# Matmul pieces laid beside a convolution and its LayerNorm, and weight sums on VectorE, in a one-core encoder layer

## The chip, the cores and the metric

The kernel runs on one core of a Trainium2 chip. The metric is the time of one execution on the device in microseconds (us). Engine names are those of the profile: PE is TensorE (matmuls), PEld its weight loads, DVE VectorE, ACT ScalarE, POOL GpSimd, SP the engine that issues most DMAs (`nc.sync`). A DMA that POOL issues (`G.dma_start` with `accum_op`) adds what it reads to what lies at its destination.

## The reference

One layer of a bidirectional encoder, S = 1024 positions, D = 1024, all in float32:

```
h  = rmsnorm(x);  P = h @ w_in                   # 8192 columns, split among the mixers
a  = glu(P[conv]);  a = depthwise_conv31(a)      # 512 channels, centred, 31 taps
a  = silu(layernorm(a)) @ pw_w                   # 512 -> 1024
o  = bidirectional_gated_scan(q, v, z_f, z_b)    # 8 heads of 128, chunks of 64
b  = (rmsnorm(o) * silu(og)) @ o_w
x  = x + (sigmoid(gA) * a + sigmoid(gB) * b) @ w_out
x  = x + (silu(dwconv3(h2 @ w_gate)) * (h2 @ w_up)) @ w_down    # h2 = rmsnorm(x), 2816 wide
out = rmsnorm(x)
```

## The kernel before

**Matmuls.** Every float32 product is three matmuls: each operand is split into a rounded high part and a rest (`split`, L121: ACT copies the high part, DVE subtracts it), and `mm3` (L146 to L148) adds high by high, rest by high and high by rest in one PSUM bank. A matmul is 128x128 weights by 512 positions; the two halves of the positions are `half` 0 and 1.

**Pair jobs.** Two columns of weights at a time are multiplied in Strassen's manner: seven products in place of eight, each of twelve matmuls, in the order 1, 2, 6, 7, 5, 4, 3 (`pair_job`, L316). For this the weights have to be added up first. `rows` (tile `wr`) is a column's weights, `col` (tile `sw`) gets the sum of both columns' upper parts, and then `wr` is changed in place by two sums (`sums`, L340). The function `add` (L329) makes these: for the first pair (`first`) DVE does, with the second column's weights loaded as another `wr`; for all others POOL issues an accumulating DMA. The order of weights is: products 1 and 2 split from `rows` as loaded (tile `wp`), 7 and 5 from `col` (tile `wq`), 6 and 3 from `rows` after the sums (tile `wp` again), 4 from a fourth part (tile `w`). A pair's results leave PSUM by DVE: (0, 0) after product 2 from bank `tr`, (1, 1) after product 5 (`ev<-su,mm`), (1, 0) after product 4 (`ev<-sc,su`), (0, 1) after product 3. ACT copies three products aside (`su`, L385). Product 3 is written to the same bank `mm` from which (1, 1) is read.

**Buffers.** `wr` has two, `sw` one, `wp` four, `wq` three, `su` four, the matmul bank `mm` three, `sc` and `tr` two each, `ob` one.

**Order.** What PE does is in the order in which the program emits it. The matmuls of a stream of jobs are generators that yield after six matmuls, here called a piece; `Stream.fill(n)` emits the next n pieces (fractions add up). A pair has 14 pieces, the 16 pairs of the input projection 224. The order on the other engines is a scheduler's, from the emitted order, the buffers and its own estimates.

**Around the change.** `s_pairs` is the stream of the 16 pairs (`in_pair`, L765). The depthwise convolution (`conv_steps`, L962) is 4 groups of channels by 31 taps, each tap one DVE instruction of 128x1024 (L970 or L973); after each, `CONV_FILL` pieces are emitted. Sums of the convolution (`acc`) go out to DRAM by `d_cv` and come back by `cx`. Then comes the LayerNorm, once for each half of the positions: six pieces, then the mean (PE L1000), DVE takes it off (L1002), six pieces, squares on ACT (L1006), sums of them (L985, L987), the variance (PE L546, a DVE copy to `r` at L550, POOL's L527 and L528, four small scalings of an identity on ACT, L535), `fill(3)`, the spread over partitions (PE L536, ACT L537), then scale, offset, silu and the split to `ch` (L1013 to L1017), and 14 pieces. The eight pointwise jobs (`conv_pw_w`) of that half are put in at the head of the queue, behind those of the half before. What is left is drained at the end (L1028).

**The FFN.** Its 22 pairs (`ffn_job`, L1580) use the same `pair_job`, `late=True`, the first of them with `now`, which takes its sums earlier. All their sums are by POOL's DMAs.

Of the kernel before, what the change touches and what calls it, by code (L numbers as in the profile page):

```python
# [17 lines left out]

P = 128
FILL = 1.37  # L20
CONV_FILL = 1.6
NPAIRS = 16
LN_FILL = 6
LN_LAST = 14
GLU_FIRST = 4
# [20 lines left out]
def tile_hybrid_encoder(  # L46
# [84 lines left out]
    def raw_w(src, nk):  # L131
        t = mp.tile([P, nk, P], F32, tag="wr", name=nm("wr"), bufs=2)
        nc.sync.dma_start(t, src)
        return t
# [178 lines left out]

        return prep, run

    def pair_job(src0, src1, nk, acts, wpool, pool, evac, su=4, first=False, late=False, now=False):  # L316

        def steps(w):
            def both(src, alt, late=late):
                hi, lo = split(w_page(2 * nk, alt), w_page(2 * nk, alt), src, V, late)
                return [(hi[:, :nk], lo[:, :nk]), (hi[:, nk:], lo[:, nk:])]

            def add(o, a):  # L329
                if first:  # L330
                    V.tensor_tensor(o, o, a, op=ALU.add)
                else:
                    G.dma_start(o, a, accum_op=ALU.add)  # L333

            rows = raw_w(src0, 2 * nk)
            col = wpool.tile([P, 2 * nk, P], F32, tag="sw", name=nm("sw"), bufs=1)
            nc.sync.dma_start(col[:, :nk], src0[:, :nk])
            nc.sync.dma_start(col[:, nk:], src1[:, :nk])
            add(col, raw_w(src1, 2 * nk) if first else src1)
            def sums():  # L340
                add(rows[:, :nk], col[:, nk:])
                add(rows[:, nk:], rows[:, :nk])

            def quadrant():
                a22 = pool.tile([P, nk, P], F32, tag="w4", name=nm("w4"), bufs=1)
                nc.sync.dma_start(a22, src1[:, nk:])
                return a22

            if now:
                w[1], w[2] = both(rows, None, False)  # L350
                sums()
                yield 0
                w[6], w[3] = both(rows, None, False)
                yield 1
                a22 = quadrant()
                yield 2
                w[7], w[5] = both(col, pool)
                yield 4
            else:
                yield 4  # L360
                w[1], w[2] = both(rows, None)
                sums()
                a22 = quadrant()
                yield 6
                w[7], w[5] = both(col, pool)
                yield 3
                w[6], w[3] = both(rows, None)
                yield 3
            one = w_page(2 * nk, pool)
            w[4] = split(one[:, :nk], one[:, nk:], a22, V, late)  # L370

        def prep():
            w = Weights(steps)
            return w if late else w.all()

        def run(w):
            def product(i, acc, fresh=True):
                for k in range(nk):
                    mm3(acc, w[i], acts(i)[k], k, fresh and k == 0, k == nk - 1, not fresh)
                    if k % 2 == 1 or k == nk - 1:  # L380
                        yield

            def copy(acc):
                t = page(pool, "su", su)
                A.copy(t, acc)  # L385
                return t

            row, b2, col = bank("mm"), bank("tr"), bank("sc")
            yield from product(1, row)
            p1 = copy(row)  # L390
            yield from product(2, b2)
            evac(0, 0, b2, p1, ALU.add)
            yield from product(6, row, False)
            u2 = copy(row)
            yield from product(7, col)
            p7 = copy(col)
            yield from product(5, row, False)
            evac(1, 1, p7, row, ALU.subtract)
            yield from product(4, col, False)
            evac(1, 0, col, u2, ALU.subtract)  # L400
            yield from product(3, row, False)
            evac(0, 1, row)

        return prep, run
# [360 lines left out]
    def in_pair(n):  # L765
        (c0, e0), (c1, e1) = todo[2 * n], todo[2 * n + 1]
        evs = (e0, e1)
        return pair_job(
            in_cols(c0),
            in_cols(c1),  # L770
            NK2,
            lambda i: ht[i],
            p1,
            p1,
            lambda e, *quadrant: evs[e](*quadrant),
            first=n == 0,
        )

    gate = {}
# [176 lines left out]


    jobs = collections.deque(in_pair(n) for n in range(1, NPAIRS))
    jobs.appendleft((lambda: w_pair0, pair0[1]))
    s_pairs = Stream(run_jobs(jobs, 4))  # L960
# [19 lines left out]
    for _ in conv_steps():  # L980
        s_pairs.fill(CONV_FILL)

# [8 lines left out]
    for half in range(2):  # L991
        xs = []
        for j in range(NCW):
            if j % 2 == 0:
                both = p1.tile([P, 2, H], F32, tag="ca", name=nm("cx"), bufs=2)
            nc.sync.dma_start(both[:, j % 2, :], d_cv[j][half])
            xs.append(both[:, j % 2, :])
        s_pairs.fill(LN_FILL)
        mean = bank("ob")
        T.matmul(mean, ones_m, total(xs, tmp()), start=True, stop=True)  # L1000
        for t in xs:
            V.scalar_tensor_tensor(t, mean, -1.0 / CW, t, op0=ALU.mult, op1=ALU.add)  # L1002
        s_pairs.fill(LN_FILL)
        sqs = [tmp() for _ in xs]
        for sq, t in zip(sqs, xs):
            A.activation(sq, t, AF.Square)  # L1006
        rstd = rstd_over_partitions(total(sqs, sqs[0]), CW, "ob", tmp())
        next(rstd)
        s_pairs.fill(3)
        rs = next(rstd)  # L1010
        ca = []
        for j, xn in enumerate(xs):
            V.tensor_tensor(xn, xn, rs, op=ALU.mult)  # L1013
            V.tensor_scalar(xn, xn, vec("lnw", j), vec("lnb", j), op0=ALU.mult, op1=ALU.add)
            A.activation(xn, xn, AF.Silu)
            both = gp0.tile([P, 2, H], F32R, tag="gl", name=nm("ch"), bufs=NCW)
            ca.append(split(both[:, 0, :], both[:, 1, :], xn, V))  # L1017
        s_pairs.fill(LN_LAST)
        at = 0
        while at < len(jobs) and jobs[at] in pw_jobs:  # L1020
            at += 1
        for i in range(ND):
            job = std_job(
                w_cols(conv_pw_w, 0, NCW, i * P), NCW, lambda k, hf, ca=ca: ca[k], store(d_a[i]), (half,)
            )
            pw_jobs.append(job)
            jobs.insert(at + i, job)
# [542 lines left out]
    class Later:  # L1570


        pool = None
# [6 lines left out]
    def ffn_job(j):  # L1580
        val = [None, None]

        def gated(hf):
            o, g = hf * H, gp[j % 2]
            c = tmp()
            pin(A.activation(c, g[:, o : o + H], AF.Identity, scale=vec("fdw", j), bias=vec("fdb", j)))
            for k in (1, 2):
                V.scalar_tensor_tensor(  # L1588
                    c,
                    g[:, o + k : o + k + H],  # L1590
                    vec("fdw", k * NF + j),
                    c,
                    op0=ALU.mult,
                    op1=ALU.add,
                )
            pin(A.activation(c, c, AF.Silu))
            V.tensor_tensor(c, c, rstd2[hf], op=ALU.mult)
            V.tensor_tensor(val[hf], val[hf], c, op=ALU.mult)
            nc.sync.dma_start(d_g[j][hf], val[hf])

        def evac(e, half, x0, x1=None, op=None):
            if e == 1:
                val[half] = page(up, "ft", 8)
                V.tensor_tensor(val[half], x0, x1, op=op)
                return
            g = gp[j % 2]
            gh = g[:, 1 + half * H : 1 + (half + 1) * H]
            if half == 0:
                V.tensor_tensor(gh, x0, x1, op=op)
                return  # L1610
            V.tensor_tensor(g[:, 1 : 1 + H], g[:, 1 : 1 + H], rstd2[0], op=ALU.mult)
            V.tensor_tensor(gh, x0, rstd2[1], op=ALU.mult)
            for hf in range(2):
                later(3 + 2 * hf, lambda hf=hf: gated(hf))

        return pair_job(
            w_cols(ffn_w_up, 0, ND, j * P),
            w_cols(ffn_w_up, 0, ND, DFF + j * P),
            NK2,
            lambda i: h2[i],  # L1620
            fw,
            up,
            evac,
            late=True,
            now=j == 0,
        )

    s_out = Stream(
# [258 lines left out]
```

## Time and profile before

| | us |
|---|---|
| median of 3 runs | 1806.72 (1804.62 to 1811.66) |
| the profiled execution | 1809.07, its span 1807.3 |
| taps L970 and L973, first to last start | 84.1 to 333.5 (L973) |
| mean of the first half (L1000) | 408.55 |
| mean of the second half (L1000) | 438.46 |
| first matmul on `ch` (pointwise) | 450.30 |

The profile is of one execution, and its times are from the start of its span. A row of a timeline has the start, the duration, the engine, the source line, the operation, what it writes and reads, and in brackets how long the engine was idle before it and what released it. Rows of the waits' view have the total, the number and the longest. L-numbers are lines of the kernel before; those of the changed kernel are one higher from line 22 on.

### The profile page before, as it was taken

To read this page: it belongs to the slowest core of one execution; us is meant where nothing else is said; L and a number is where in the kernel's file an instruction comes from. 1 tells how busy PE (TensorE), PEld (TensorE's weight loads), DVE (VectorE), ACT (ScalarE), POOL (GpSimd) and SP (SyncE) were. 2 spreads that over 40 slices of the span, in tenths; PEclk is the share of its full clock that TensorE was granted. 3 is DMA by queue.
4 is the path that set the end of the run, shared out by engine and by line. 5 is a ranking of instruction groups with operands and counts; after the bars stand their busy time and mean duration, and the time that the engine had idled before them with its cause. 6 is when DMAs were issued, how large, how long until landed. Compare 5 with 4: busy or idle time off the path is not lost.

```text
span 1807.3 us, 33410 instructions
## 1 busy us (share of the span) xinstructions
PE 1753.0 (97%) x13546; PEld 1426.5 (79%) x13546; DVE 1240.4 (69%) x1842; ACT 783.1 (43%) x1488; POOL 186.1 (10%) x185
## 2 busy tenths in 40 slices
PE   8989999998999999999999999899999999999997
PEld 6878887776787777788888888688888888888885
DVE  5599999535479999999445566566766766545355
ACT  7343332234555666665442245334434434422123
POOL 2201111110000000011000002111111111000000
PEclk9999999999999999999999999999999999999999
DMA  8657878774653333342267566776766766534233
GB/s 284 217 148 181 193 178 198 183 161 125 209 181 101 119 119 119 119 135 86 89 209 211 182 207 196 148 158 143 154 152 146 151 147 133 161 97 128 82 92 135
DMA packets 317873, 279.16 MB, mean 154 GB/s; under 512 B 14606, under 2 KB 241174, under 8 KB 317718
## 3 DMA queue, kind: packets, MB, share of 16 engines
q1 hardware_dynamic: 268582, 238.21, 42.3%
q0 software_dynamic: 49136, 38.80, 14.9%
q8 instruction: 106, 1.74, 0.4%
q14 instruction: 49, 0.40, 0.1%
HBM read 184.95 MB, written 72.61 MB: 143 GB/s over the span
## 4 chain that ended last, share of the span: by engine, by line
PE 72%; DVE 14%; DMA 8%; issue 4%; ACT 1%; POOL 1%; SPq 0%; POOLq 0%; DVEq 0%; ACTq 0%
PE mm L146 18%; PE mm L147 17%; PE mm L148 17%; DVE acc L973 3%; PE sc L146 3%; PE sc L148 3%; PE sc L147 3%; PE ob L1071 3%; DMA sw<-in_w_in_dram 2%; DMA wr<-wr 1%; DVE wp L122 1%; DMA wr<-sw 1%; PE tr L146 1%; PE tr L147 1%; PE tr L148 1%
## 5 line engine op out<-in xcount | busy, mean ns | idle before, releaser
L146 PE MATMUL mm<-hx,wp 128*128 128x512 f32 x1152 | 464.2, 403 | 12.1 <-ACT su L385 5.8
L148 PE MATMUL mm<-hx,wp 128*128 128x512 f32 x1152 | 451.7, 392 | 1.7 <-DVE wp L122 1.6
L147 PE MATMUL mm<-hx,wp 128*128 128x512 f32 x1152 | 450.9, 391 | 0.8 <-issue 0.8
L122 ACT CAST wp<-wr 128x1024 fp32r<-128x1024 f32 (+2 forms) x157 | 144.1, 918 | 352.8 <-PE mm L147 237.0
L146 PEld LDWEIGHTS mm<-hx,wp 128*128 128x128 f32 x1152 | 217.2, 189 | 63.6 <-DVE ev L735 7.4
L148 PEld LDWEIGHTS mm<-hx,wp 128*128 128x128 f32 x1152 | 217.1, 188 | 51.3 <-DVE wp L122 3.6
L147 PEld LDWEIGHTS mm<-hx,wp 128*128 128x128 f32 x1152 | 217.6, 189 | 41.9 <-issue 0.5
L122 DVE TENSOR_TENSOR wp<-wr,wp 128x1024 fp32r<-128x1024 f32 (+2 forms) x155 | 164.7, 1063 | 110.6 <-ACT wp L122 103.7
L973 DVE SCALAR_TENSOR_TENSOR acc<-gl,v_b,acc 128x1024 f32<-128x1024 f32 x120 | 149.2, 1280 | 0.5
L1738 DVE TENSOR_TENSOR xr<-mm,xr 128x512 f32<-128x512 f32 x48 | 33.2, 691 | 72.9 <-PE mm L148 72.9
L333 POOL DMA_DIRECT2D wr<-sw x37 | 32.8, 887 | 432.8 <-DVE wp L122 239.9
L122 ACT CAST wq<-sw 128x1024 fp32r<-128x1024 f32 x38 | 40.0, 1052 | 64.6 <-PE mm L147 30.3
L1588 DVE SCALAR_TENSOR_TENSOR tm<-gp,v_a,tm 128x512 f32<-128x512 f32 x88 | 66.0, 750 | 2.0
L385 ACT COPY su<-mm 128x512 f32<-128x512 f32 x76 | 44.0, 579 | 51.6 <-PE mm L148 50.4
L146 PE MATMUL mm<-hy,wp 128*128 128x512 f32 x152 | 60.5, 398 | 4.5 <-ACT su L385 4.5
L147 PE MATMUL mm<-hy,wp 128*128 128x512 f32 x152 | 60.2, 396 | 0.0
L146 PE MATMUL tr<-hx,wp 128*128 128x512 f32 x152 | 59.6, 392 | 0.0
L146 PE MATMUL sc<-hy,wq 128*128 128x512 f32 x152 | 59.6, 392 | 0.0
L148 PE MATMUL mm<-hy,wp 128*128 128x512 f32 x152 | 59.5, 392 | 0.0
L148 PE MATMUL sc<-hy,wq 128*128 128x512 f32 x152 | 59.5, 391 | 0.0
L148 PE MATMUL tr<-hx,wp 128*128 128x512 f32 x152 | 59.2, 389 | 0.0
L147 PE MATMUL tr<-hx,wp 128*128 128x512 f32 x152 | 59.1, 389 | 0.0
(363 smaller groups left out, 3545.1 us busy)
## 6 DMA issues: line engine op xcount, KB each, us to landing
wr<-in_w_in_dram SPq DMA_DIRECT2D x52, 512.0 KB, 4.4
sw<-in_ffn_w_up_dram SPq DMA_DIRECT2D x44, 256.0 KB, 3.4
sw<-in_ffn_w_up_dram POOLq DMA_DIRECT2D x22, 512.0 KB, 8.4
wr<-in_ffn_w_up_dram SPq DMA_DIRECT2D x22, 512.0 KB
d_g<-ft SPq DMA_DIRECT2D x44, 256.0 KB, 2.0
wr<-sw POOLq DMA_DIRECT2D x37, 256.0 KB, 3.2
wr<-wr POOLq DMA_DIRECT2D x37, 256.0 KB, 3.6
sw<-in_w_in_dram SPq DMA_DIRECT2D x32, 256.0 KB, 3.3
```

Source lines behind the costliest of these rows:

```text
L122: parts = A.copy(hi, src), eng.tensor_tensor(lo, src, hi.bitcast(F32), op=ALU.subtract)
L146: T.matmul(acc, whi[:, k, :], ahi, start=first, stop=False, skip_group_check=again)
L147: T.matmul(acc, whi[:, k, :], alo, start=False, stop=False, skip_group_check=again)
L148: T.matmul(acc, wlo[:, k, :], ahi, start=False, stop=last, skip_group_check=again)
L333: G.dma_start(o, a, accum_op=ALU.add)
L385: A.copy(t, acc)
L973: V.scalar_tensor_tensor(acc, g[:, k : k + S], tap(k), acc, op0=ALU.mult, op1=ALU.add)
L1071: T.matmul(o[g : g + 32], l[:, g : g + 32], r, start=start, stop=stop)
L1588: V.scalar_tensor_tensor(c, g[:, o + k : o + k + H], vec("fdw", k * NF + j), c, op0=ALU.mult, op1=ALU.add,)
L1738: V.tensor_tensor(xr[i][half], acc, xr[i][half], op=ALU.add)
```

## The change

`CONV_FILL` goes from 1.6 to 1.3. The parameter `first` of `pair_job` becomes `own`; it holds for the first pair, for the 12th to 16th (`OWN_FROM = 11`, counted from 0) and for the second pair of the FFN (`j == 1`), which then add up their weights by DVE and load the second column's weights as a tile `wr`. Between the variance and the spread of the LayerNorm stand five pieces, not three.

```diff
--- before.py
+++ after.py
@@ -18,8 +18,9 @@
 
 P = 128
 FILL = 1.37
-CONV_FILL = 1.6
+CONV_FILL = 1.3
 NPAIRS = 16
+OWN_FROM = 11
 LN_FILL = 6
 LN_LAST = 14
 GLU_FIRST = 4
@@ -313,7 +314,7 @@
 
         return prep, run
 
-    def pair_job(src0, src1, nk, acts, wpool, pool, evac, su=4, first=False, late=False, now=False):
+    def pair_job(src0, src1, nk, acts, wpool, pool, evac, su=4, own=False, late=False, now=False):
 
 
 
@@ -327,7 +328,7 @@
                 return [(hi[:, :nk], lo[:, :nk]), (hi[:, nk:], lo[:, nk:])]
 
             def add(o, a):
-                if first:
+                if own:
                     V.tensor_tensor(o, o, a, op=ALU.add)
                 else:
                     G.dma_start(o, a, accum_op=ALU.add)
@@ -336,7 +337,7 @@
             col = wpool.tile([P, 2 * nk, P], F32, tag="sw", name=nm("sw"), bufs=1)
             nc.sync.dma_start(col[:, :nk], src0[:, :nk])
             nc.sync.dma_start(col[:, nk:], src1[:, :nk])
-            add(col, raw_w(src1, 2 * nk) if first else src1)
+            add(col, raw_w(src1, 2 * nk) if own else src1)
             def sums():
                 add(rows[:, :nk], col[:, nk:])
                 add(rows[:, nk:], rows[:, :nk])
@@ -773,7 +774,7 @@
             p1,
             p1,
             lambda e, *quadrant: evs[e](*quadrant),
-            first=n == 0,
+            own=n == 0 or n >= OWN_FROM,
         )
 
     gate = {}
@@ -1006,7 +1007,7 @@
             A.activation(sq, t, AF.Square)
         rstd = rstd_over_partitions(total(sqs, sqs[0]), CW, "ob", tmp())
         next(rstd)
-        s_pairs.fill(3)
+        s_pairs.fill(5)
         rs = next(rstd)
         ca = []
         for j, xn in enumerate(xs):
@@ -1623,6 +1624,7 @@
             evac,
             late=True,
             now=j == 0,
+            own=j == 1,
         )
 
     s_out = Stream(
```

How this moves instructions is shown at three places; what order a kernel's engine has there is printed for both kernels.

The first is DVE, in the convolution, in the third pair (pair 2): `ev` are evictions, `wp` and `wq` splits of weights, `acc` taps. Before:

```order
L735 TENSOR_TENSOR ev_1761<-tr_1706,su_1721 128x512
L122 TENSOR_TENSOR wp_1743<-wr_1736,wp_1742 128x1024
L973 SCALAR_TENSOR_TENSOR acc_1419<-gl_362,v_b,acc_1419 128x1024
L973 SCALAR_TENSOR_TENSOR acc_1930<-gl_353,v_b,acc_1930 128x1024
L973 SCALAR_TENSOR_TENSOR acc_1419<-gl_362,v_b,acc_1419 128x1024
L973 SCALAR_TENSOR_TENSOR acc_1930<-gl_353,v_b,acc_1930 128x1024
L973 SCALAR_TENSOR_TENSOR acc_1419<-gl_362,v_b,acc_1419 128x1024
L735 TENSOR_TENSOR ev_1809<-su_1794,mm_1705 128x512
L122 TENSOR_TENSOR wq_1751<-sw_1738,wq_1750 128x1024
L973 SCALAR_TENSOR_TENSOR acc_1419<-gl_362,v_b,acc_1419 128x1024
L735 TENSOR_TENSOR ev_1826<-sc_1707,su_1778 128x512
L122 TENSOR_TENSOR wq_1758<-w_302_1748,wq_1758 128x512
```

After, from the same `wp` split on (between it and the eviction of bank `tr` now stands one tap):

```order
L123 TENSOR_TENSOR wp_1748<-wr_1741,wp_1747 128x1024
L974 SCALAR_TENSOR_TENSOR acc_1419<-gl_362,v_b,acc_1419 128x1024
L974 SCALAR_TENSOR_TENSOR acc_1833<-gl_353,v_b,acc_1833 128x1024
L974 SCALAR_TENSOR_TENSOR acc_1419<-gl_362,v_b,acc_1419 128x1024
L974 SCALAR_TENSOR_TENSOR acc_1833<-gl_353,v_b,acc_1833 128x1024
L974 SCALAR_TENSOR_TENSOR acc_1419<-gl_362,v_b,acc_1419 128x1024
L123 TENSOR_TENSOR wq_1756<-sw_1743,wq_1755 128x1024
L974 SCALAR_TENSOR_TENSOR acc_1419<-gl_362,v_b,acc_1419 128x1024
L123 TENSOR_TENSOR wq_1763<-w_302_1753,wq_1763 128x512
L974 SCALAR_TENSOR_TENSOR acc_1419<-gl_362,v_b,acc_1419 128x1024
L736 TENSOR_TENSOR ev_1814<-su_1799,mm_1709 128x512
L974 SCALAR_TENSOR_TENSOR acc_1419<-gl_362,v_b,acc_1419 128x1024
```

The eviction `ev<-su,mm` stood behind five taps after the `wp` split; now both `wq` splits stand ahead of it too, and three more taps, one of them ahead of the `wp` split.

The second is DVE in the FFN, where the second pair's sums are made. Before, with no sum on DVE:

```order
L122 TENSOR_TENSOR hy_12598<-ft_12514,hy_12597 128x512
L122 TENSOR_TENSOR hy_12602<-tm_12457,hy_12601 128x512
L122 TENSOR_TENSOR wq_12613<-w_1856_12508,wq_12613 128x512
L122 TENSOR_TENSOR wp_12617<-wr_12556,wp_12616 128x1024
L122 TENSOR_TENSOR hy_12639<-ft_12568,hy_12638 128x512
L122 TENSOR_TENSOR hy_12643<-ft_12570,hy_12642 128x512
L1604 TENSOR_TENSOR ft_12666<-su_12630,mm_12499 128x512
L1611 TENSOR_TENSOR gp_12493<-gp_12493,rs_11740 128x512
L122 TENSOR_TENSOR hy_12659<-ft_12572,hy_12658 128x512
L122 TENSOR_TENSOR hy_12663<-ft_12574,hy_12662 128x512
L1604 TENSOR_TENSOR ft_12680<-sc_12501,su_12605 128x512
```

After:

```order
L123 TENSOR_TENSOR hy_12610<-ft_12524,hy_12609 128x512
L332 TENSOR_TENSOR sw_12568<-sw_12568,wr_12571 128x1024
L123 TENSOR_TENSOR hy_12614<-tm_12467,hy_12613 128x512
L123 TENSOR_TENSOR wq_12625<-w_1861_12518,wq_12625 128x512
L123 TENSOR_TENSOR wp_12629<-wr_12566,wp_12628 128x1024
L332 TENSOR_TENSOR wr_12566<-wr_12566,sw_12568 128x512
L1605 TENSOR_TENSOR ft_12678<-su_12642,mm_12509 128x512
L332 TENSOR_TENSOR wr_12566<-wr_12566 128x512
L123 TENSOR_TENSOR hy_12651<-ft_12580,hy_12650 128x512
L123 TENSOR_TENSOR hy_12655<-ft_12582,hy_12654 128x512
L1612 TENSOR_TENSOR gp_12503<-gp_12503,rs_11750 128x512
L1605 TENSOR_TENSOR ft_12692<-sc_12511,su_12617 128x512
```

The three L332 rows are the sums: one into `sw` ahead of the second pair's last `hy` split of that group, two into `wr` behind the `wp` split, and the first of the `ft` evictions stands between these.

The third is PE in the LayerNorm's second half. Before, the mean (L1000), the variance (L546), the spread (L536) and the first pointwise matmuls follow one another:

```order
L146 MATMUL mm_3566<-hx_946,wp_3452 128x512
L147 MATMUL mm_3566<-hx_947,wp_3452 128x512
L148 MATMUL mm_3566<-hx_946,wp_3453 128x512
L1000 MATMUL ob_3709<-tm_3710,ones_m 128x512
L546 MATMUL ob_3731<-ones_m,tm_3719 128x1 x4
L536 MATMUL ob_3740<-tm_3741,ones_m 128x512
L146 MATMUL mm_3784<-ch_3600,wp_3774 128x512
L147 MATMUL mm_3784<-ch_3600,wp_3774 128x512
```

After, around the variance (here of line 547):

```order
L149 MATMUL sc_3484<-hy_1102,wq_3390 128x512
L147 MATMUL sc_3484<-hy_1124,wq_3389 128x512
L148 MATMUL sc_3484<-hy_1125,wq_3389 128x512
L149 MATMUL sc_3484<-hy_1124,wq_3390 128x512
L547 MATMUL ob_3568<-ones_m,tm_3556 128x1 x4
L147 MATMUL mm_3482<-hy_1068,wq_3389 128x512
L148 MATMUL mm_3482<-hy_1069,wq_3389 128x512
L149 MATMUL mm_3482<-hy_1068,wq_3390 128x512
```

The variance now has matmuls of a pair on both sides of it, and thirty of them follow it ahead of the spread.

## The prediction

> **What bounds the kernel now.** I read the page first, then what TensorE (PE) waited for, then the timelines of the engines at each of those waits.
>
> ```profile
> span 1807.3 us, 33410 instructions
> PE 1753.0 (97%) x13546; PEld 1426.5 (79%) x13546; DVE 1240.4 (69%) x1842; ACT 783.1 (43%) x1488; POOL 186.1 (10%) x185
> PE 72%; DVE 14%; DMA 8%; issue 4%; ACT 1%; POOL 1%; SPq 0%; POOLq 0%; DVEq 0%; ACTq 0%
> ```
>
> PE is busy for 97% of the span and carries the chain. The change neither adds nor removes a matmul, so it can only touch the time in which PE waits, or runs at a lower clock because it waited. The second view says where those waits are:
>
> ```profile
> PE mm L146 <- ACT su L385: 10.3, 4, 5.8
> PE mm L146 <- DVE ev L735: 4.7, 4, 3.5
> ```
>
> (Total us, times, the longest.) L146 behind ACT's `su` (L385) is a pair's third product in its order (number 6), and L146 behind the eviction `ev` L735 its last one. Beside them stand the LayerNorm's variance (L546) and its spread (L536), one wait each, shown below. All of these lie at places that the diff touches. Two stretches:
>
> ```profile
> core 0: us, PE busy (x) PEld busy (x) DVE busy (x) ACT busy (x) POOL busy (x), PEclk, DMA share, GB/s
> 200.00:240.00 40.00, 40.00 (x178) 33.14 (x177) 39.46 (x38) 16.11 (x23) 7.86 (x7) 1.00 0.82 189
> 438.50:454.50 16.00, 8.14 (x22) 5.50 (x21) 7.79 (x14) 6.12 (x13) 1.20 (x2) 0.68 0.34 99
> ```
>
> In the convolution PE is full, but so is VectorE (DVE): 39.46 of 40 us. In the norm's second half PE does 8 us of work in 16, at a granted clock of 0.68.
>
> **Term 1, the norm's second half.** Matmuls are laid out in pieces of six; the 16 pairs have 16 × 14 = 224. At 1.6 pieces a tap, 124 taps use 198; the first half then takes 6 + 6 + 3 + 14 = 29, and 198 + 29 = 227 is more than there are: the second half finds none. At 1.3 the taps use 161, the first half 6 + 6 + 5 + 14 = 31, and its mean comes at piece 167; the second half begins at 192, and its 6 + 6 + 5 fit below 224. What the empty half costs now:
>
> ```profile
> 438.46 1.02 PE L1000 MATMUL ob<-tm,ones_m 128*128 128x512 f32 x2
> 444.40 1.87 PE L546 MATMUL ob<-ones_m,tm 128*128 128x1 f32 x8 [4.93 <-DVE tm L987]
> 449.21 2.08 PE L536 MATMUL ob<-tm,ones_m 128*128 128x512 f32 x2 [2.94 <-ACT tm L535]
> 450.30 1.42 PE L146 MATMUL mm<-ch,wp 128*128 128x512 f32 x1
> 454.43 0.40 PE L148 MATMUL mm<-ch,wp 128*128 128x512 f32 x1
> ...
> 446.56 0.20 POOL L527 TENSOR_SCALAR r<-r 128x4 f32<-128x4 f32 x1 [26.34 <-DVE r L550]
> 446.84 1.01 POOL L528 TENSOR_TENSOR r<-r,mhalf 128x4 f32<-128x4 f32 x1
> 447.88 1.28 ACT L535 ACTIVATE tm<-ident,r 128x128 f32<-128x128 f32 x4 [5.00 <-POOL r L528]
> ...
> 357.08 0.39 PE L146 MATMUL tr<-hx,wp 128*128 128x512 f32 x1
> 359.57 0.39 PE L148 MATMUL tr<-hx,wp 128*128 128x512 f32 x1
> ```
>
> The last two rows, 11 matmuls apart, give the step at full clock: 2.49 / 11 = 0.227 us, so a piece is 1.36 and a pair of 84 matmuls 19.05. From 438.46 to 454.43, where the step is short again, are 15.97 us. The work in them at full clock is 1.02 + 1.87 / 2 + 2.08 / 2 + 9 × 0.227 = 5.0. **About 11 us go.** What is late next? Six pieces (8.2 us) lie between mean and variance, where the chain takes 444.40 − 438.46 = 5.9; five (6.8) between variance and spread, where it takes 449.21 − 444.40 = 4.8. Both are covered while DVE is free; but DVE now also has a pair's splits and sums in that place. In the first half the copy to `r` stands behind a sum and a split of pair 13, 1.2 us each. Piece 167 is one piece ahead of pair 12, which starts at 357.08 − 12 × 0.227 = 354.4 now; so the mean stands at 353, the variance at 353 + 8.2 + 1 = 362, its result a us later, `r` at about 365, and behind GpSimd (1.29) and ACT (1.28) the operand at 368. PE asks for it at 353 + 11 × 1.36 + 2 = 370, or 368.8 if it lost nothing before.
>
> There the Trainium skill has a rule against the change: "SBUF — State Buffer", section "SBUF: two separate sides", says that GpSimd and a VectorE operation with two SBUF inputs lock a port pair against each other, the loser blocked for a whole instruction. The new sums are such operations and may stand beside GpSimd's rstd; by the rule each of its two operations could wait out a sum (1.2 us), the rstd 2.4 late, and the time 3 us above my sum. The trace itself:
>
> ```profile
> 1118.71 0.93 POOL L527 TENSOR_SCALAR r<-r 128x4 f32<-128x4 f32 x1
> 1119.72 1.46 POOL L528 TENSOR_TENSOR r<-r,mhalf 128x4 f32<-128x4 f32 x1
> ```
>
> The same two operations take 2.47 us beside a busy DVE and 1.29 beside an idle one (446.56). So an rstd beside DVE is late by 1.2 us, of which at least 0.8 is covered: 0 to 0.4 us a half. By that the rule's direction holds, at half its size.
>
> **Term 2, the sums of pairs 12 and 14.** (Pairs are counted from 0.)
>
> ```profile
> 362.23 0.80 PE L146 MATMUL mm<-hy,wp 128*128 128x512 f32 x1 [2.27 <-ACT su L385]
> 366.64 0.40 PE L146 MATMUL sc<-hy,wq 128*128 128x512 f32 x1
> 402.96 0.50 PE L146 MATMUL mm<-hy,wp 128*128 128x512 f32 x1 [0.79 <-ACT su L385]
> ...
> 360.16 1.04 ACT L122 CAST wp<-wr 128x1024 fp32r<-128x1024 f32 x1 [7.70 <-DMA wr<-wr]
> ```
>
> ACT's cast of the summed weights waits for the last accumulating DMA (`wr<-wr`), with the `su` copy that PE wants queued behind it. From 359.57 to 366.64 are 13 steps: 7.07 against 2.95, so 4.1 us lost; pair 14 loses 0.79 and a slow step, 1.1. With DVE's adds the three accumulating transfers of a pair, one behind the other, are gone. Their price, and the last transfer's:
>
> ```profile
> L331 DVE TENSOR_TENSOR sw<-sw,wr x1: 1219/1219/1219, 113.5 to 113.5; 128x1024 f32<-128x1024 f32 x1
> L331 DVE TENSOR_TENSOR wr<-wr,sw x1: 687/687/687, 116.4 to 116.4; 128x512 f32<-128x512 f32 x1
> wr<-wr POOLq DMA_DIRECT2D x37, 256.0 KB, 3.6
> ```
>
> 1.22 + 2 × 0.69 = 2.6 us of DVE a pair, beside 19.05 us of PE; behind the taps DVE is not full. I cost it at nothing and the gain at **5.2 us** (from 3, if `r` or an eviction is held up instead, to 5.2).
>
> **Term 3, the convolution.** The new density puts more taps ahead of each pair's work in DVE's order. What stands there before:
>
> ```profile
> 165.83 6.07 DVE L973 SCALAR_TENSOR_TENSOR acc<-gl,v_b,acc 128x1024 f32<-128x1024 f32 x5
> 171.81 0.69 DVE L735 TENSOR_TENSOR ev<-su,mm 128x512 f32<-128x512 f32 x1
> 172.41 1.22 DVE L122 TENSOR_TENSOR wq<-sw,wq 128x1024 fp32r<-128x1024 f32 x1
> 172.78 0.40 PE L146 MATMUL mm<-hx,wp 128*128 128x512 f32 x1
> 192.76 0.50 PE L146 MATMUL mm<-hx,wp 128*128 128x512 f32 x1 [0.61 <-DVE ev L735]
> 311.49 0.80 PE L146 MATMUL mm<-hx,wp 128*128 128x512 f32 x1 [3.47 <-DVE ev L735]
> ...
> 306.31 0.69 DVE L985 TENSOR_TENSOR tm<-cx 128x512 f32<-128x512 f32 x1 [3.24 <-DMA cx<-d_cv]
> ```
>
> The eviction of 171.81 empties the bank into which pair 2's last product goes. Now a tap, the `wq` split, a tap, the second `wq` split and a tap come ahead of it: three taps (five last 171.81 − 165.83 = 5.98, so 1.2 each), 1.2, and 0.7 as for other 128x512 adds, some 5.5 in all. It is ready at about 178 in place of 172.5; PE reaches the product at 172.78, so it waits 5.1, and runs at about half clock after that (362.23: 0.43 a step for 3.4 us, after a wait of 2.27): 1.6 more. **6.7 lost.** Further on both orders have 11 taps a pair, with a slack of 1 to 2 us as at 192.76. Regained is the wait at 311.49, which came from an add (306.31) that waited for its load ahead of an eviction; that add now stands ahead of a weight split with slack: 3.47 and its slow steps, 5.1, and 1.2 of smaller gaps. Net **−0.4** (from −5.5, if an eviction is held up there all the same, to +6.3, if the first wait is hidden).
>
> The mean does not wait instead. Its last inputs follow the last tap:
>
> ```profile
> 333.52 1.28 DVE L973 SCALAR_TENSOR_TENSOR acc<-gl,v_b,acc 128x1024 f32<-128x1024 f32 x1
> ```
>
> Store, load and three adds put the sums at about 343 (333.52 + 1.3, the 3.2 us waited for such a load at 306.31, as much for the store, 2 for the adds), while PE reaches the mean at 353. Fewer pairs stand among the taps, so the last tap comes, if anything, earlier.
>
> **Term 4, the FFN's second pair.**
>
> ```profile
> 1138.62 0.39 PE L148 MATMUL tr<-hx,wp 128*128 128x512 f32 x1
> 1144.82 0.79 PE L146 MATMUL mm<-hx,wp 128*128 128x512 f32 x1 [5.82 <-ACT su L385]
> 1151.06 0.39 PE L146 MATMUL sc<-h,wq 128*128 128x512 f32 x1
> ...
> 1137.85 0.85 POOL L333 DMA_DIRECT2D wr<-wr  x1 [2.67 <-DMA wr<-sw]
> 1156.09 0.83 POOL L333 DMA_DIRECT2D wr<-wr  x1 [2.62 <-DMA wr<-sw]
> ```
>
> 16 steps take 12.44 where 3.63 would do: 8.8 lost. With the sums on DVE the weights are split by about 1137.6, before PE asks. But the third pair still sums by DMA. Its last sum was issued at 1156.09 and, like the second's (PE ran on 1144.82 − 1137.85 = 7.0 after the issue), would let PE go at about 1163.1; PE now asks 19.05 after 1138.62, at 1157.7. Its column load should start 3.5 earlier, since the buffer is read out earlier: 1159.6, a wait of 2 us. **+7** (2.5 if the load is no earlier, 8.8 if the wait is hidden).
>
> For this wait the trace and a page differ. The Trainium skill, "TensorE: Matmul & The Clock Gate", section "What's actually happening", has the clock fall only after an idle window of some 3.4 us. By it no slow steps would follow a 2 us wait; the row at 362.23 shows them after 2.27. By the page term 4 stays at 7; by the trace a wait a little longer than the 2 us makes it 5.4. I leave 7 and keep 5.4 for the range.
>
> **Term 5.** The last pair now comes behind the 16 pointwise jobs, whose two-piece products give DVE and ACT less time apiece; with spread and entry I charge 2 us (0 to 5).
>
> **Sum.** 11 + 5.2 − 0.4 + 7 − 2 = 20.8. The profiled execution took 1809.07 (span 1807.3 and 1.8 around it), so 1788.3; it lay 2.35 above the median of 1806.72, which gives 1785.9. I take **1787**, between.
>
> **Rivals.**
> 1. *Nothing is given back:* the eviction in pair 2 is hidden (+6.7) and the third FFN pair finds its sums (+1.8): 1787 − 8.5 = 1778.5. The slack at 192.76, under 0.6 us, is against it.
> 2. *Waits move on:* the third FFN pair takes back 6.3 of 8.8 (−4.5), the spread comes late in both halves with its slow steps (3.2 + 1.7 = −5), the last pair's entry costs 3 more: 1799.
> 3. *Without effect in the norm:* DVE, with a pair's sums and splits in the chain, lengthens it as much as the pieces cover; 11 stays: 1798. Against it: 7.79 us of DVE in the 16 us of that stretch.
> 4. *Slower:* DVE is the bound of the convolution (39.46 of 40 us). If it is late at the last product not in one pair but in five, four more at 6.7 each are 26.8: 1787 + 26.8 = 1814. It decides once DVE is later than 2.7 us, a product of twelve steps, behind the pair's own order. The equal count of taps a pair speaks against it.
>
> **How the numbers follow.** Half a per cent, 9 us, is what a measurement can tell. Forecast 0.62, rival 1 0.12, rival 2 0.14, rival 3 0.06, rival 4 0.06. The range, 1777 to 1801, takes in all but rival 4 and little of the ends. Faster means below 1797.7: the forecast, rival 1, and somewhat under half of rivals 2 and 3, 0.83; the same: the rest of these, 0.11; slower: rival 4, 0.06.
>
> **What would show it.** Right: the second half's rows L546 and L536 have no wait, their clock is 1.00, and the span around them is shorter by 11; L146 behind `su` is gone from pairs 12 and 14 and stands in the FFN's third pair with 1 to 3 us, not in the second; L735 has a new wait near 173 of some 5, and none near 311. Wrong: waits at L735 in several pairs between 190 and 330, a wait at L1000 for its sums, or the sums' adds standing ahead of the copy to `r` for longer than five pieces last.

## The result, and the profile after

Six runs of the changed kernel gave a median of 1789.11 us (1787.32 to 1795.05), six of the kernel before 1808.26; the ratio is 0.9899, with a 95% interval of 0.9884 to 0.9914. The forecast of 1787 was right to 2 us, and its side too. The profiled execution, 1795.05 with a span of 1793.0, is the slowest of the six; the spans of the two profiles, 1807.3 and 1793.0, differ by 14.3 us, not by the 19 of the medians. The page, and the waits of PE (total us, times, longest), of the changed kernel; its lines are one higher:

```profile
span 1793.0 us, 33359 instructions
PE 1747.9 (97%) x13546; PEld 1423.5 (79%) x13546; DVE 1253.2 (70%) x1860; ACT 784.0 (44%) x1488; POOL 165.7 (9%) x167
...
PE mm L147 <- DVE ev L736: 7.6, 3, 4.7
PE mm L147 <- ACT su L386: 4.3, 3, 1.7
PE mm L149 <- DVE wp L123: 2.7, 3, 1.0
```

The waits of the norm (4.9 and 2.9 before) are gone, those for `su` are down from 10.3 to 4.3 us, those for the evictions are up from 4.7 to 7.6. DVE has 12.8 us more work and POOL 20 less. The norm's halves, as stretches of the same view that was shown of before:

```profile
core 0: us, PE busy (x) PEld busy (x) DVE busy (x) ACT busy (x) POOL busy (x), PEclk, DMA share, GB/s
356.50:380.00 23.50, 23.50 (x106) 18.86 (x105) 16.56 (x25) 11.64 (x21) 2.02 (x2) 1.00 0.47 145
401.50:421.00 19.50, 19.50 (x87) 15.55 (x86) 7.98 (x14) 6.84 (x14) 1.20 (x2) 1.00 0.30 100
```

In both PE is busy throughout, at full clock. Next, the rows of PE's timeline where it waits in the convolution (first fence) and in the FFN (second):

```profile
176.84 0.80 PE L147 MATMUL mm<-hx,wp 128*128 128x512 f32 x1 [4.73 <-DVE ev L736]
255.82 0.50 PE L147 MATMUL mm<-hx,wp 128*128 128x512 f32 x1 [0.84 <-DVE ev L736]
296.27 0.80 PE L147 MATMUL mm<-hx,wp 128*128 128x512 f32 x1 [2.03 <-DVE ev L736]
```

```profile
1131.08 0.40 PE L147 MATMUL sc<-h,wq 128*128 128x512 f32 x1
1187.58 0.50 PE L147 MATMUL mm<-hx,wp 128*128 128x512 f32 x1 [1.22 <-ACT su L386]
1247.71 0.50 PE L147 MATMUL mm<-hx,wp 128*128 128x512 f32 x1 [1.70 <-ACT su L386]
1248.48 0.77 PE L149 MATMUL mm<-hx,wp 128*128 128x512 f32 x1
1249.05 0.63 PE L147 MATMUL mm<-hx,wp 128*128 128x512 f32 x1
```

PE runs the same products in both kernels, so the start of one product in the two profiles, subtracted, says where the time went:

| product | before | after | after − before |
|---|---|---|---|
| last product of pair 2 | 172.78 | 176.84 | +4.1 |
| last product of pair 10 | 332.46 | 336.48 | +4.0 |
| first matmul of the scans (L1199, now L1200) | 526.09 | 514.68 | −11.4 |
| spread of the FFN's norm | 1125.55 | 1114.40 | −11.2 |
| FFN's second pair, `sc` | 1150.10 | 1131.08 | −19.0 |
| FFN, `sc` of a pair near 1500 | 1517.29 | 1503.27 | −14.0 |

The convolution loses 4, the pairs and norm behind it gain 15.4, the FFN's second pair some 8, and 5 of these are given back in its fifth and eighth pair.

### The profile page after: what moved, and what is told of

The parts are those of the page before. It is cut to its first block, busy times and chain, and to the rows that moved or that the text cites. A ratio compares the mean times of both kernels' runs of the same rounds, so it can differ in the third digit from the quotient of the medians.

```text
span 1793.0 us, 33359 instructions
## 1 busy us (share of the span) xinstructions
PE 1747.9 (97%) x13546; PEld 1423.5 (79%) x13546; DVE 1253.2 (70%) x1860; ACT 784.0 (44%) x1488; POOL 165.7 (9%) x167
## 4 chain that ended last, share of the span: by engine, by line
PE 73%; DVE 13%; DMA 8%; issue 5%; ACT 1%; POOL 0%; SPq 0%; POOLq 0%; DVEq 0%; ACTq 0%
PE mm L147 18%; PE mm L149 18%; PE mm L148 18%; PE ob L1072 3%; DVE acc L974 3%; PE sc L149 2%; PE sc L147 2%; PE sc L148 2%; DMA wr<-wr 2%; DMA wr<-sw 1%; PE tr L147 1%; PE tr L149 1%; PE tr L148 1%; DVE qF L1061 1%; DMA sw<-in_w_in_dram 1%
## 5 line engine op out<-in xcount | busy, mean ns | idle before, releaser
L334 POOL DMA_DIRECT2D wr<-sw x31 | 27.5, 886 | 378.9 <-DVE wp L123 207.2
```

## The experiments

There were twelve experiments, on ten kernels: e0 and e8 are the changed kernel, and e6 and e11 are one kernel. Two questions stood: is the gain in the norm the density's, as term 1 of the prediction priced it, and what gives the FFN's 5 us back? For each experiment the table has the ratio to the kernel before on the same chip and, from its one profile, the start of the scans (which sums up convolution, pairs and norm) and the time from the FFN norm's `ob` matmuls (L546/L547) to the last transpositions (L1788/L1790), all in us:

| kernel | ratio, 95% interval | scans start | FFN |
|---|---|---|---|
| before | 1 | 526.1 | 680.5 |
| changed | 0.9899 (0.9884 to 0.9914) | 514.7 | 678.1 |
| e0, changed | 0.9929 (0.9913 to 0.9945) | 514.6 | 677.2 |
| e8, changed | 0.9913 (0.9897 to 0.9929) | 512.2 | 671.9 |
| e1, 1.6 again | 0.9953 (0.9935 to 0.9970) | 522.8 | 677.1 |
| e2, density alone | 1.0057 (1.0037 to 1.0077) | 532.4 | 680.8 |
| e3, no FFN sums | 0.9958 (0.9943 to 0.9973) | 513.3 | 678.3 |
| e4, pair sums alone | 0.9986 (0.9969 to 1.0003) | 521.3 | 679.3 |
| e5, three pieces | 0.9942 (0.9923 to 0.9961) | 522.2 | 671.9 |
| e6, two densities | 0.9905 (0.9873 to 0.9938) | 510.3 | 672.2 |
| e11, two densities | 0.9884 (0.9867 to 0.9900) | 512.5 | 674.7 |
| e7, every third FFN pair | 0.9926 (0.9907 to 0.9945) | 515.0 | 674.2 |
| e9, no pair sums | 0.9960 (0.9948 to 0.9972) | 521.7 | 675.3 |
| e10, all mended | 0.9926 (0.9912 to 0.9940) | 511.9 | 678.7 |

**The changed kernel again (e0, e8).** No edit.

> The changed kernel once more, unchanged. Theory: what the instructions' order fixes comes back at its place (waits of the last product for the eviction L736 of 4.7 us near 172, 0.8 near 255 and 2.0 near 294 us), while the FFN's waits for ACT's su (1.2 us in its fifth pair, 1.7 in its eighth) are late DMA sums and move from one execution to the next: a time of 1787 to 1792, and other pairs in the profile. Rival: the FFN's waits are fixed too and stand in the fifth and eighth pair again, 1795 in the profiled execution.

> The changed kernel a third time, beside the two others of this call. Theory: 0.990 to 0.993 of the kernel before; the waits for L736 at their places, FFN waits for su in none to two pairs, not the same as in the other two profiles.

The waits that hang on DVE's order came back: 4.6 and 2.5 us in e0, 4.8 and 1.7 in e8; that near 255, of 0.8, in neither. Of the FFN's two waits, e0 has none in the fifth pair and one of 2.81 in the eighth, as before, and its time (median 1794.05, the profiled execution 1795.44) lies with the rival and not with the 1787 to 1792 expected. e8 decides against the rival: it has neither wait, and its FFN is 5 to 6 us shorter than the other two. Runs of one kernel on one chip spread as far (1786.61 to 1795.41 in e8).

The FFN is the same in eight of the profiles. Four have no wait for `su` in it (e5, e6, e8, e11) and take 671.9 to 674.7 us there; the four that have one take 675.3 to 678.1.

**One part undone: the density (e1).**

```diff
-CONV_FILL = 1.3
+CONV_FILL = 1.6
```

> The changed kernel with 1.6 pieces a tap as before; sums by VectorE, and five pieces in the norm's middle, stay. Theory (the density alone covers the norm's second half, and alone delays the evictions in the convolution): the wait at 172 goes and that near 307 comes back, a gain of 4 us; the second half finds no pieces and loses 11: 1789 + 11 - 4 = 1796. Rival (the sums by VectorE are what helps the norm, or the density costs nothing in the convolution): 1785 to 1789.

1796.58 us, as the theory had it. Its scans start 8 to 11 us later than in the changed kernel, the wait near 308 is back (3.52 us), that at 172 gone, and the norm's second half waits again, as in the kernel before:

```profile
441.39 1.87 PE L547 MATMUL ob<-ones_m,tm 128*128 128x1 f32 x8 [4.76 <-DVE tm L988]
446.19 2.07 PE L537 MATMUL ob<-tm,ones_m 128*128 128x512 f32 x2 [2.94 <-ACT tm L536]
```

So DVE's sums and five pieces ahead of the spread do not help the second half where the stream has run out; the density that leaves pieces for it does. The expectation set it against 1789; the changed kernel beside it had 1794.05, so the difference in whole runs, 2.5, is less than the forecast 7, within what the two intervals leave open (0.0024 ± 0.0024 of 1806, 0 to 9 us).

**One part alone: the density (e2).**

```diff
-CONV_FILL = 1.6
+CONV_FILL = 1.3
```

(in the kernel before)

> The kernel before with 1.3 pieces a tap alone; all sums but the first pair's by DMA, three pieces in the norm's middle. Theory: 11 us gained in the norm's second half, 4 lost in the convolution, the waits for sums in the pairs 12 and 14 (5.2 us) and in the FFN's second pair (8.8) stay: 1808 - 11 + 4 = 1801, and up to 3 more if three pieces (4.1 us) are too few for the spread. Rival (without VectorE's sums the norm gains nothing): 1812.

A miss: 1817.04, 11 us **slower** than before, where 1801 was expected and the rival had 1812. The second half of the norm no longer waits for itself, but new waits stand where the pairs and the norm now meet. Three of them on PE, then DVE and POOL at the first of these and ACT at the third:

```profile
372.75 2.08 PE L536 MATMUL ob<-tm,ones_m 128*128 128x512 f32 x2 [3.58 <-ACT tm L535]
384.01 0.50 PE L146 MATMUL mm<-hx,wp 128*128 128x512 f32 x1 [3.26 <-DVE ev L735]
488.08 0.65 PE L146 MATMUL mm<-hy,wp 128*128 128x512 f32 x1 [3.15 <-ACT wp L122]
...
364.96 0.16 DVE L550 COPY r<-ob 128x4 f32<-128x4 f32 x1
...
369.10 0.90 POOL L333 DMA_DIRECT2D wr<-sw  x1 [7.08 <-DMA sw<-in_w_in_dram]
370.07 0.19 POOL L527 TENSOR_SCALAR r<-r 128x4 f32<-128x4 f32 x1
370.35 1.04 POOL L528 TENSOR_TENSOR r<-r,mhalf 128x4 f32<-128x4 f32 x1
...
486.99 1.04 ACT L122 CAST wp<-wr 128x1024 fp32r<-128x1024 f32 x1 [4.15 <-DMA wr<-wr]
```

The variance is copied to `r` at 365.1, but POOL takes it up only at 370.07: in its queue stood a pair's accumulating DMA, waiting 7.08 us for the sum before it to land. In the changed kernel POOL has no DMA there and starts when `r` is there (rows further on). So the sums by DVE serve the norm too: they clear POOL's queue for the rstd. That is the first wait only. The one of 3.15 us is ACT's cast of the last pair's weights, which waits for that pair's own DMA sum. The one of 3.26 has nothing to do with sums: e5 below, with DVE's sums, has it too. PE also waited 3.50 at 396.42, for a split that stood behind an add of the second half's inputs, which had waited 3.41 for its load.

**The sums and the pieces (e4, e9, e5).** e4 is the kernel before with `OWN_FROM` for the pairs alone; e9 is the changed kernel without it; e5 is the changed kernel with three pieces:

```diff
# e4: CONV_FILL = 1.6, fill(3), FFN own=False, and
+            own=n == 0 or n >= OWN_FROM,
# e9
-OWN_FROM = 11
+OWN_FROM = 16
# e5
-        s_pairs.fill(5)
+        s_pairs.fill(3)
```

> The kernel before with the sums of the 12th to 16th pair by VectorE, alone (1.6 pieces a tap, three in the norm's middle, FFN sums by DMA). Theory, after the density alone came out 11 us slower: the parts do not add up, since GpSimd's rstd stands in one queue with its accumulating DMAs; alone, these sums give the 5 us of the waits in the pairs 12 and 14: ratio 0.997, about 1800 on a chip where the kernel before takes 1806. Rival (the sums alone give most of the gain, the density adds nothing): 0.991 or less.

> The changed kernel without VectorE's sums in the 12th to 16th pair (density, five pieces and the FFN's pair stay). Theory: in the kernel with the density alone, GpSimd's rstd stood behind an accumulating DMA's wait, and the pairs among the norm waited for their own sums; five pieces cover a part of the spread's wait, the rest stays: 9 to 15 us slower than the changed kernel, ratio about 0.998 to 1.001. Rival (the five pieces alone mend what the density alone lost): 0.990 to 0.993 as the changed kernel.

> The changed kernel with three pieces in place of five between variance and spread. Theory: the operand of the spread takes about 6 us from the variance where pair 13's sum and split stand ahead of r, three pieces cover 4.1: the spread of the first half waits 2 to 3 us and runs 1 to 2 us of slow steps, the second half waits under 1: 4 to 5 us slower than the changed kernel, ratio to the kernel before about 0.995. Rival (the five pieces are not needed): as the changed kernel, 0.990 to 0.993.

e4 gives 3.4 us by the medians and 2.5 by the ratio, whose interval reaches to no gain; its profile gives 4.8 at the scans' start, where term 2 said 5.2. Its rival is out. e9 gives 1799.85, 0.996: under the 9 to 15 us of the expectation (8 beside e8 on the same chip, with intervals that do not touch), but not the rival's 0.990 to 0.993. Its POOL row stands as e2's does, at 372.24 behind the DMA of 371.26, its spread waits 2.53, and PE waits 2.17 for the last pair's sum; it does not wait for the eviction near 384. e5 came out at 0.9942, near the 0.995 expected, but for another reason: its spread waits 0.38 only. DVE of e5 (first fence) and of e8 with five pieces (second), behind the spread of the first half, shows why:

```profile
379.22 1.29 DVE L123 TENSOR_TENSOR ch<-cx,ch 128x512 fp32r<-128x512 f32 x2
380.42 0.68 DVE L123 TENSOR_TENSOR wq<-w,wq 128x512 fp32r<-128x512 f32 x1
381.02 0.68 DVE L123 TENSOR_TENSOR ch<-cx,ch 128x512 fp32r<-128x512 f32 x1
381.62 0.54 DVE L1015 TENSOR_SCALAR cx<-cx,v_a 128x512 f32<-128x512 f32 x1
382.08 0.68 DVE L736 TENSOR_TENSOR ev<-su,mm 128x512 f32<-128x512 f32 x1
```

```profile
371.67 0.69 DVE L736 TENSOR_TENSOR ev<-su,mm 128x512 f32<-128x512 f32 x1 [4.64 <-PE mm L149]
372.45 1.23 DVE L123 TENSOR_TENSOR wq<-sw,wq 128x1024 fp32r<-128x1024 f32 x1
373.60 1.29 DVE L1014 TENSOR_TENSOR cx<-cx,tm 128x512 f32<-128x512 f32 x2
```

With three pieces the pair's eviction `ev<-su,mm` stands behind the norm's scaling and splitting, and PE waits 3.71 us for it at 382.82; with five it comes out ahead of them. The two pieces work less by covering the spread than by putting an eviction ahead of the norm in DVE's order. The scans start 7 to 10 us later in e5 than in the changed kernel; that its runs are but a few slower fits its profile's FFN, which has no wait for `su`.

Put together, by the start of the scans, one profile for each but the last:

| density | sums in pairs | pieces | start of the scans |
|---|---|---|---|
| 1.6 | DMA | 3 | 526.1 |
| 1.6 | DVE | 3 | 521.3 |
| 1.6 | DVE | 5 | 522.8 |
| 1.3 | DMA | 3 | 532.4 |
| 1.3 | DMA | 5 | 521.7 |
| 1.3 | DVE | 3 | 522.2 |
| 1.3 | DVE | 5 | 512.2 to 515.1 |

Alone the density loses 6; with DVE's sums it loses 1 (522.2 against 521.3); with both of the others it gains 8 to 11 (against 522.8). At 1.3 the sums and the two pieces mend about 10 each. With the five pieces and no sums by DVE it lies 4 ahead of the kernel before; the density of 1.6 with DMA sums and five pieces was not run.

**The FFN (e3, e7).**

```diff
# e3
-            own=j == 1,
+            own=False,
# e7
-            own=j == 1,
+            own=j % 3 == 1,
```

> The changed kernel with the FFN's second pair summed by DMA again. Theory (the wait in the second pair was worth 8.8, and part of it is taken back in later FFN pairs by their own late sums): 8.8 come back in the second pair and the waits of the fifth and eighth pair go: 1789 + 8.8 less 2 to 5 = 1793 to 1796. Rival (the later waits have nothing to do with it): they stay and the time is 1798.

> The changed kernel with VectorE's sums in every third FFN pair (the 2nd, 5th, 8th and so on), not in the 2nd alone. Theory: the later FFN waits are GpSimd's chain of accumulating DMAs, which has no slack left once the second pair no longer holds PE up; a pair without DMA sums lets the chain catch up, so no FFN pair waits for su: 3 to 5 us faster than the changed kernel, ratio 0.988 to 0.990. Rival (the sums on VectorE only add work and new waits): no gain, or up to 5 us slower.

e3 came out at 1797.86, above the 1793 to 1796 expected and at the rival's 1798. But the changed kernel beside it was at 1794.05 and not at 1789, so the difference is 3.8 by the medians and 5 by the ratios, whose intervals leave 1 to 9 open; the runs lean to the theory's 4 to 7 and do not rule out the rival's 9. The profile has the wait of 5.34 us in the second pair again and none behind it, as the theory had it. POOL's chain shows why the waits move on. In e0 (the first fence below) 7.95 us pass in one pair and 10.95 in another from the issue of the column sum to that of the next (the difference of two starts; the column sum lands 0.6 us ahead of the second), and the eighth pair's last sum, issued at 1239.00, comes too late by 2.81. In e3 (second fence) the chain keeps a step of 19.2 to 19.6 us, and PE, late by the second pair's wait, asks later for every sum. In e8 (third fence), which has no wait, the column sum is released by DVE and not by the transfer before it: there the chain waits for the engines.

```profile
1166.80 1.57 POOL L334 DMA_DIRECT2D sw<-in_ffn_w_up_dram  x1 [5.36 <-DMA sw<-in_ffn_w_up_dram]
1174.75 0.87 POOL L334 DMA_DIRECT2D wr<-sw  x1 [6.38 <-DVE wp L123]
...
1203.64 1.57 POOL L334 DMA_DIRECT2D sw<-in_ffn_w_up_dram  x1 [5.37 <-DMA sw<-in_ffn_w_up_dram]
1214.59 0.87 POOL L334 DMA_DIRECT2D wr<-sw  x1 [9.38 <-DVE tm L1598]
...
1239.00 0.84 POOL L334 DMA_DIRECT2D wr<-wr  x1 [3.14 <-DMA wr<-sw]
```

```profile
1162.78 0.85 POOL L334 DMA_DIRECT2D wr<-wr  x1 [2.59 <-DMA wr<-sw]
1182.36 0.84 POOL L334 DMA_DIRECT2D wr<-wr  x1 [2.67 <-DMA wr<-sw]
1201.52 0.85 POOL L334 DMA_DIRECT2D wr<-wr  x1 [2.63 <-DMA wr<-sw]
```

```profile
1179.79 1.56 POOL L334 DMA_DIRECT2D sw<-in_ffn_w_up_dram  x1 [5.24 <-DVE gp L1613]
1198.60 1.57 POOL L334 DMA_DIRECT2D sw<-in_ffn_w_up_dram  x1 [5.52 <-DVE gp L1613]
1217.96 1.56 POOL L334 DMA_DIRECT2D sw<-in_ffn_w_up_dram  x1 [4.93 <-DVE gp L1613]
```

e7's profile has no wait for `su` in the FFN, as expected, but neither have four of the eight profiles without this edit, and the runs gained nothing: 0.9926 where 0.988 to 0.990 was expected. With sums in more pairs another wait came, 1.26 us for the eviction `ft` near 1411; e10 shows it five times.

**Versions that might be better (e6, e11, e10).** Two densities, again 161 pieces; e10 adds e7's edit and sums the norm's inputs from the last to the first:

```diff
# e6 and e11
-    for _ in conv_steps():
-        s_pairs.fill(CONV_FILL)
+    for n, _ in enumerate(conv_steps()):
+        s_pairs.fill(1.6 if n < 80 else 0.75)
# e10, besides
-        T.matmul(mean, ones_m, total(xs, tmp()), start=True, stop=True)
+        T.matmul(mean, ones_m, total(xs[::-1], tmp()), start=True, stop=True)
```

> The changed kernel with 1.6 pieces a tap for the first 80 taps and 0.75 for the last 44: again 161 pieces, so the norm finds the same pieces, but VectorE's order in the convolution is that of the kernel before. Theory: the waits for L736 near 172, 255 and 294 go (9 us with their slow steps), the one near 308 comes back (5): 4 us faster than the changed kernel, ratio 0.988 to 0.990. Rival (the waits in the convolution come from the lower density itself, whatever the order): no gain.

> The two densities again, with five rounds. Theory: the convolution's gain over the changed kernel (2 to 4 us at the norm) is there, and the FFN's waits for su decide between 1786 and 1792: ratio 0.988 to 0.992. Rival (the gain is within the spread of the chips): 0.991 to 0.993 as the changed kernel.

> Two densities (1.6 for 80 taps, then 0.75), VectorE's sums in every third FFN pair, and the norm's four inputs added from the last to the first, so that no add waits for its load in the midst of the convolution. Theory: beside the gain of the two densities the wait near 308 (5 us with slow steps) goes, and the FFN has no waits for su: 8 to 11 us faster than the changed kernel, ratio 0.984 to 0.987. Rival (what is mended in one place is waited for in the next): as the two densities alone, 0.988 to 0.991.

e6 and e11 have no wait near 172, and the old one near 308 is back (3.51 and 3.76 us). Up to the 80th tap, at 250, both the density and DVE's order are those of the kernel before, so this does not tell the two apart. Behind it the density is 0.75, lower than 1.3; in e6 the `wq` split (288.50) stands behind the eviction (287.90) again, as in the kernel before, and PE does not wait near 294 (0.71 us in e11 at 289.52). So a low density alone does not make that wait; what differs is the order. Their scans start at 510.3 and 512.5. With 1787.62 and 1788.28, 0.9905 and 0.9884, they are as fast as the changed kernel or a few us faster: e11's interval lies below e0's, but it overlaps the first and, barely, e8's, and e6's lies over all three. Neither ran beside the changed kernel on one chip at one time. e10, where all was to come together, is no better than the changed kernel: 1793.83, 0.9926 where 0.984 to 0.987 was expected. The add's wait went, but PE now waits 2.11 near 309 and, here, 2.50 for an eviction behind two taps and the second of two sums:

```profile
331.91 0.73 PE L147 MATMUL mm<-hx,wp 128*128 128x512 f32 x1 [2.50 <-DVE ev L736]
...
328.06 0.69 DVE L332 TENSOR_TENSOR wr<-wr 128x512 f32<-128x512 f32 x1
328.66 2.60 DVE L974 SCALAR_TENSOR_TENSOR acc<-gl,v_b,acc 128x1024 f32<-128x1024 f32 x2
331.18 0.68 DVE L736 TENSOR_TENSOR ev<-su,mm 128x512 f32<-128x512 f32 x1
```

And the FFN waits for `ft` five times (5.1 us in all), each time with two of DVE's sums among what stands ahead of that eviction. So its rival held, and by more than it said.

## Why the prediction was right, point by point

- *Term 1, 11 us in the norm's second half*: the waits went, PE is full there at clock 1.00, and of the 15.4 gained behind the convolution about 12 are left for it when term 2's 4.8 is taken off and term 5's 1.5 added. But the step from 161 pieces among the taps to 11 us gained holds only with the other two edits: alone the density cost 11 us (e2). The prediction had looked at POOL's rstd beside DVE, not at POOL's queue ahead of it, and priced the five pieces for the spread only, not for the eviction behind it (e5). As the other edits were in the kernel too, the sum was not hurt.
- *Term 2, 5.2 us*: 4.8 by e4.
- *Term 3, −0.4*: the mis-sized one; it measured −4.2 (the 4.0 of the table, and 0.2 by which the changed kernel was ahead at the first tap). The 6.7 lost in pair 2 came nearly as forecast (a wait of 4.73 for 5.1, with steps of 0.43 us behind it), and the wait at 311 went. The step that failed is "further on both orders have 11 taps a pair, with a slack of 1 to 2 us": at 255 and 296 two more evictions were late, by 0.84 and 2.03 us and the second's slow steps, 0.9 and 3.5 us in all by the starts of the same matmuls. At 296 a `wq` split stands ahead of the eviction, besides five taps, as in pair 2. The rival of late evictions in four more pairs, which was also the prediction's first sign of being wrong, was partly true: in two, at a third of its 6.7 each.
- *Term 4, +7*: the second pair gave 8.5 (from −10.5 just ahead of it to −19.0 against before), near the forecast 8.8. The wait expected in the third pair did not come; its last sum was issued at 1139.25, 5.7 us earlier against the start of the FFN and not 3.5. The same give-back came later, in the fifth and eighth pair in the profile (5.0 with slow steps), in none in e8: 3.5 to 8.5 in net, with 7 inside.
- *Term 5, 2 us*: about 1.5: 1.02 for a pointwise split at 425, and 0.3 in the last pair.
- The rstd beside DVE: the rows below, of the changed kernel, first half with DVE's sums (L332) and second. The two operations took 2.11 us from start to end where DVE's two sums ran and 1.29 where it was idle, 0.8 later and not 1.2, and the spread did not wait. Each operation is longer by about what was left of a running sum, which is how an exclusive lock would look; it is argued from these rows, not tested.

```profile
368.02 0.53 POOL L528 TENSOR_SCALAR r<-r 128x4 f32<-128x4 f32 x1 [52.20 <-DVE r L551]
368.64 1.49 POOL L529 TENSOR_TENSOR r<-r,mhalf 128x4 f32<-128x4 f32 x1
412.03 0.19 POOL L528 TENSOR_SCALAR r<-r 128x4 f32<-128x4 f32 x1 [41.90 <-DVE r L551]
412.31 1.01 POOL L529 TENSOR_TENSOR r<-r,mhalf 128x4 f32<-128x4 f32 x1
...
367.81 0.69 DVE L332 TENSOR_TENSOR wr<-wr,sw 128x512 f32<-128x512 f32 x1
368.54 0.69 DVE L332 TENSOR_TENSOR wr<-wr 128x512 f32<-128x512 f32 x1
```

In the profiled execution the errors add up to 20.8 − 3.8 (term 3) − 3.5 (the FFN, 8.5 less 5.0 for 7) + 1.2 (15.4 for the 14.2 of terms 1, 2 and 5) = 14.7, and the trace shows 14.3. The median is 6 us better than that execution; e8's profile, with no FFN wait for `su`, has 6.2 us less in the FFN. So that the forecast met the median to 2 us is in part luck: between the two profiled executions its sum promised 20.8 us and the traces show 14.3, short in terms 3 and 4, and what made up for it is that other executions have less of the FFN's waits. The last is argued from e8's profile and the other three without such a wait; the faster five of the six executions were not traced.

What stays open: why a column sum takes 8 us in one pair and 11 in another, and with it why the FFN's waits differ from one execution to the next; whether the two densities are truly faster than one; and what a density of 1.6 with five pieces and DMA sums would give.

## What to carry to other kernels

Terms of a sum read off one trace need not add up: ask of each edit which queue it empties or fills for the others, and try each alone (here the density lost 6 us alone and gained 8 to 11 beside the sums and the pieces). Where a fixed chain of transfers runs at the pace of the engine that needs it, a wait taken away at its head can turn up further on, since that wait was the chain's slack; here it did in four of the eight profiles with that edit. On an engine that works through its instructions in order and is nearly full, look at what stands ahead of the one eviction that frees a bank; that order can cost more than the work added.

## What the hardware showed unexpectedly

How long PE waited does not settle what its clock does next. In the changed kernel the step behind the waits of 2.03 us at 296.27 and 1.70 at 1247.71 was 0.43 us, at a granted clock of 0.50, for about 3 us. Behind 1.72 at 295.61 (e8), 2.11 at 309.76 (e10) and 3.26 at 384.01 (e2) it stayed at 0.23, with the clock at 1.00. The 1.6 us of slow steps that the prediction adds to a wait were there in some executions and not in others; no run here shows what decides it.

A queue of GpSimd that holds a DMA waiting for another DMA held a 1.3 us computation behind it for 5 us (365.1 to 370.07).
